# Turning written keys and normed outputs through DRAM and VectorE's 32x32 blocks, where TensorE's transposes stood

## The chip, the cores and the metric

The kernel runs on one core of one Trainium2 chip. A core has four engines that compute (TensorE, called PE in the profile, with its weight loads as PEld; VectorE, DVE; ScalarE, ACT; GpSimd, POOL), SyncE (SP), which here only issues DMAs, and 16 DMA engines that serve all queues. The metric is the device time of one execution in microseconds (us); lower is better. Beside it, a profiled execution gives the start and length of each instruction and of each DMA packet.

## What is computed

One layer of a hybrid decoder trunk over 512 tokens and 2048 channels, float32. After an RMSNorm, one product with `w_in` gives r, k, v, two small LoRA streams, a gate g, and the streams of a pooling group. The part that the change touches is the RWKV-7 group, 16 heads of 64 channels:

```python
def step(S, inp):                                   # per token, per head
    r_t, w_t, k_t, v_t, kk_t, a_t = inp
    sa = einsum('bhvk,bhk->bhv', S, -kk_t)
    S = S * w_t[:, :, None, :] + sa[..., None] * (kk_t * a_t)[:, :, None, :] + v_t[..., None] * k_t[:, :, None, :]
    y_t = einsum('bhvk,bhk->bhv', S, r_t)
...
y = head_group_norm(y, ln_w, ln_b)                  # per head, over its 64 channels
y_rwkv = (y + bonus) * silu(g_rwkv)
```

Then the pooling group, the product with `w_out` and the residual, a gated embedding (`w_pg`, `w_ple`), and a last RMSNorm.

## The kernel before

**Two kinds of work on TensorE.** Every large product is made of three matmuls of split operands (high and low halves in fp32r), 128x128 by 128x512. These are the filler: `stream()` is a generator that yields them one by one (tiles `zr`, `zk`, `zv`, `zg` for the RWKV streams, `zb` for the pooling group, `pple` for the embedding), and `pump(n)` puts n of them into the program. From line 345 on (`pin[0] = True`) TensorE keeps program order, so the filler stands exactly where `pump` is called. Between the filler stands the recurrence.

**Pairs.** The 16 heads are taken in pairs: pair j (j = 0 to 7) is 128 channels, one tile of 128 partitions by 512 tokens. A pair's tokens are cut into 8 chunks of 64. For each pair, in program order:

- `prepare(j)` (VectorE): scaled copies `ar` (reads) and `bk` (the written keys, 128 x 1024 values, 512 KB, two per token: the value key and the removal key). `bk` is a single buffer (pool `rw`, tag "bk").
- `scores(j)` (L608): 32 matmuls `pm` of `bk` with `ar`; four masked copies `mt` (L623); four DMAs of 32 KB `nd<-mt` to DRAM (L639), and from there two DMAs `n<-nd` back as a broadcast (L644).
- `invert(j)`: 31 small VectorE steps (`tm`, `xw`, L657 and L661) that solve the triangular blocks; they start with the first `n` block and are fed two at a time into the chunk loop of pair j-1, behind an instruction of its chain (`issue_after(lead[0].ins)`). Then four DMAs `xd<-xw` and four back, to `x1` (tile `x` in the profile).
- `gather(j)` (L678): the squared-key norm, decay and rate of pair j+1; four TensorE transposes `pv` of the values; **eight transposes `pbk` of `bk`** (L699) and two ScalarE copies into `bkn`, in which the tokens lie on partitions; `pump(H4)` (8), `norm_key(j+1)`, `pump(H5)` (13); **then the pending output gate of pair j-1**; `pump(HX)` (13); then the joined visit, which closes the inverse: a VectorE transpose `y` of `x1` in 32x32 blocks (L723), the matmuls `pq`, `pmv`, `px` and ScalarE copies back into `x1` and `mv`; `pump(2 * H1)` (12).
- `recur(j)` (L753): for each chunk a matmul `py` and a VectorE sum `zs` (L784), filler, a matmul `pu` and ScalarE copies `uv`, filler, a matmul `ps` with `bkn[:, ch]` and VectorE's new state `sbd` (L806), filler. Inside chunk 0, `between()` puts 20 filler matmuls, `scores(j+1)` and more filler. At the end the outputs `ysb` (tokens on partitions) are normed by eight VectorE instructions (L851), and `finish` is put into `pending`.
- `finish`, the output gate (L854): **four TensorE transposes `pyt` of `ysb`**, ScalarE's scale and bias (L860), two VectorE products with bonus and gate (L861, L862), and a DMA `yd<-yo` issued by ScalarE. The last pair's gate stands after `pump(HE)` (40).

The order of the loop is `prepare(j+1)`, `recur(j)`, `gather(j+1)`. After the last gate the pool `rw` is closed and its memory is used anew: the tiles `yin`, `yhi`, `ylo` (from L913 on), read by the product with `w_out` (`acc_o`).

**What sets the order elsewhere.** On the engines other than TensorE, and on SP's queue, the framework orders instructions when the kernel is built, taking at each point what its model of time holds ready, the earlier in the program first; so a load can stand ahead of an older one that isn't ready. Each engine then runs its list strictly in that order. SP's queue holds all weight loads (`raw`, four buffers, L129) beside `nd`, `n`, `xd` and `x`.

Of the kernel before, what the change touches and what calls it, by code (L numbers as in the profile page):

```python
# [15 lines left out]
P = 128  # L16
# [18 lines left out]
def trunk_kernel(ctx: ExitStack, tc: tile.TileContext, x, p, norm_g, w_in, mu, w0, w_up, a0, a_up,  # L35
# [84 lines left out]
    def dp(o, i):  # L120
        return dprm[:, o + i:o + i + 1]
# [455 lines left out]
    def prepare(j):  # L577
        k_, r_, v_ = need("k", j), need("r", j), need("v", j)
        pw, ipw, tha = pws.pop(j)
        kk = kks.pop(j)  # L580
        if j + 1 < NJ:
            load_ab(j + 1)


        ar = rw.tile([P, NCH // 2, 4, C], F32, name=f"ar{j}", tag="ar", bufs=2)
        bk = rw.tile([P, NCH // 2, 4, C], F32, name=f"bk{j}", tag="bk")
        k4 = kk.rearrange("p (q c t) -> p q c t", c=2, t=C)
        pw4 = pw.rearrange("p (q c) t -> p q c t", c=2)
        i4 = ipw.rearrange("p (q c) t -> p q c t", c=2)
        kp = rw.tile([P, T], F32, name=f"kp{j}", tag="kp")  # L590
        nc.vector.tensor_scalar(kp, tha, dp(33, j), dp(41, j), ALU.mult, ALU.add)
        nc.vector.tensor_tensor(kp, kp, k_, ALU.mult)
        nc.vector.tensor_scalar(tha, tha, 0.5, 0.5, ALU.mult, ALU.add)
        nc.vector.tensor_tensor(ar[:, :, 0::3, :], r_.rearrange("p (q c t) -> p q c t", c=2, t=C),
                                pw4[:, :, :, 1:C + 1], ALU.mult)
        nc.vector.tensor_tensor(bk[:, :, 0::3, :], kp.rearrange("p (q c t) -> p q c t", c=2, t=C), i4, ALU.mult)
        nc.vector.scalar_tensor_tensor(ar[:, :, 1:3, :], k_.rearrange("p (q c t) -> p q c t", c=2, t=C), dp(89, j),
                                       pw4[:, :, :, 0:C], ALU.mult, ALU.mult)
        nc.vector.tensor_tensor(kk, kk, tha, ALU.mult)
        nc.vector.tensor_tensor(bk[:, :, 1:3, :], k4, i4, ALU.mult)  # L600
        nc.vector.scalar_tensor_tensor(kp, r_, dp(49, j), kp, ALU.mult, ALU.mult)
        kph = rw.tile([P, T], F32R, name=f"kph{j}", tag="t", bufs=4)
        kpl = rw.tile([P, T], F32R, name=f"kpl{j}", tag="t", bufs=4)
        split(kph, kpl, kp)

        st_[j] = dict(pw=pw, ar=ar, bk=bk, v_=v_, kp=(kph, kpl))

    def scores(j):  # L608
        ar, bk, v_ = (st_[j][n_] for n_ in ("ar", "bk", "v_"))
        kph, kpl = st_[j].pop("kp")  # L610

        mt = rw.tile([P, 2, 8, 2, C], F32, name=f"mt{j}", tag="mt", bufs=2)
        pm = [[psM.tile([P, T], F32, name=f"pm{j}_{par}0", tag="m"),
               psY.tile([P, T], F32, name=f"pm{j}_{par}1", tag="y")] for par in range(2)]
        for par in range(2):
            for q in range(4):
                for h in range(2):
                    rows = slice(64 * h, 64 * h + 64)
                    mm(pm[par][h][:, q * P:(q + 1) * P], bk[rows, q, 2 * par:2 * par + 2, :],
                       ar[rows, q, 2 * par:2 * par + 2, :], start=True, stop=True)  # L620
        for par in range(2):
            for h in range(2):
                nc.vector.tensor_tensor(mt[:, par, h::2, :, :],  # L623
                                        pm[par][h].rearrange("p (u a t) -> p u a t", u=4, a=2),
                                        msk[:, par:par + 2, :].unsqueeze(1).to_broadcast([P, 4, 2, C]), ALU.mult)


        ps = psM.tile([P, T], F32, name=f"pbo{j}", tag="m")
        mm(ps, blk, kph, start=True, stop=False)
        mm(ps, blk, kpl, start=False, stop=True)  # L630
        bv = rw.tile([P, T], F32, name=f"bv{j}", tag="bv", bufs=2)
        nc.vector.tensor_tensor(bv, ps, v_, ALU.mult)

        nd = dram.tile([2, 2, 8, 32, 32], F32, name=f"nd{j}", tag="nd")
        for par in range(2):
            pb = 64 * (1 - par)
            for b in range(2):
                rows = slice(pb + 32 * b, pb + 32 * b + 32)
                nc.sync.dma_start(out=nd[par, b].rearrange("u r c -> r u c"),  # L639
                                  in_=mt[rows, par, :, 1 - par, 32 * b:32 * b + 32])  # L640
        nb = []
        for i in range(2):
            t_ = rw.tile([P, 16, 32], F32, name=f"n32{j}_{i}", tag=("kk", "kp")[i])
            nc.sync.dma_start(out=t_, in_=nd[:, :, :, 16 * i:16 * i + 16, :].rearrange(  # L644
                "a b u r c -> (a b u) r c").unsqueeze(0).to_broadcast([4, 32, 16, 32]))
            nb.append(t_)
        st_[j].update(mt=mt, nb=nb, bv=bv)


    def invert(j):  # L650
# [26 lines left out]

    def gather(j):  # L678
        d = st_[j]
        bk, v_, mt = d.pop("bk"), d.pop("v_"), d["mt"]  # L680
        if j + 1 < NJ:
            prepare_key(j + 1)
            decay_and_rate(j + 1)
# [7 lines left out]
        nc.scalar.copy(uv[64:128, 1::2, :], pv[64:128])  # L691


        bkn = rw.tile([P, NCH, P], F32, name=f"bkn{j}", tag="bkn")
        for hf in range(2):
            ps = psM.tile([P, T], F32, name=f"pbk{j}_{hf}", tag="m")
            for i in range(4):
                ch = 4 * hf + i
                tr(ps[:, i * P:(i + 1) * P], bk[:, ch // 2, 2 * (ch % 2):2 * (ch % 2) + 2, :], ident)  # L699
            nc.scalar.copy(bkn[:, 4 * hf:4 * hf + 4, :], ps.rearrange("p (c n) -> p c n", n=P))  # L700

        pump(H4)

        d.update(uv=uv, bkn=bkn)
        if j + 1 < NJ:
            norm_key(j + 1)
        pump(H5)
        if pending:
            pending.pop()()
        pump(HX)  # L710

        x1 = d["x1"]
# [34 lines left out]
        nc.scalar.copy(zsp[0][64:128, :].rearrange("p (h t) -> p h t", h=2), psv[64:128, 0:2, :])  # L747
        nc.scalar.copy(mv.rearrange("p q (h t) -> p (q h) t", h=2), psv)
        d["mv"] = mv
        pump(2 * H1)  # L750


    def recur(j, work, between):  # L753
        d = st_.pop(j)
        pw, ar, mt, bv, uv, bkn, mv, x1 = (d[n_] for n_ in ("pw", "ar", "mt", "bv", "uv", "bkn", "mv", "x1"))
        hop = [0]
        HC1, HC2, HC3 = HC
        lead = [None]
# [12 lines left out]
        for ch in range(NCH):  # L771
# [8 lines left out]
            if ch > 0:  # L780
# [5 lines left out]
                step()  # L786
                pump(HC1)

            psu = psS.tile([P, T], F32, name=f"pu{j}_{ch}", tag="s")
            mm(psu[:, 0:P], x1[:, 2 * q:2 * q + 2, :], zs, start=True, stop=True)  # L790
            for h in range(2):
# [58 lines left out]
        for i in range(8):  # L850
            nc.vector.tensor_scalar(y8[:, i, :], y8[:, i, :], mvr[:, i, 0:1], rs8[:, i, :],  # L851
                                    ALU.subtract, ALU.mult)

        def finish():  # L854
            sg = need("g", j)
            ps = psM.tile([P, T], F32, name=f"pyt{j}", tag="m")
            for tt in range(NT):
                tr(ps[:, tt * P:(tt + 1) * P], ysb[:, tt, :], ident)
            yo = rw.tile([P, T], F32, name=f"yo{j}", tag="t", bufs=4)
            nc.scalar.activation(yo, ps, AF.Identity, scale=dp(57, j), bias=dp(65, j))  # L860
            nc.vector.tensor_tensor(yo, yo, bv, ALU.add)  # L861
            nc.vector.tensor_tensor(yo, yo, sg, ALU.mult)  # L862
            nc.scalar.dma_start(out=yd[j], in_=yo)

        pending.append(finish)

    HC, HT, HX = (6, 9, 9), 130, 13
    HS, HN = 5, 2
    HP = 1000
    pending = []  # L870
    need("k", 0)
    need("r", 0)
    prepare_key(0)
# [11 lines left out]
    for j in range(NJ):  # L885
# [13 lines left out]
        recur(j, invert(j + 1) if j + 1 < NJ else iter(()), between)  # L899
        if j + 1 < NJ:  # L900
            gather(j + 1)
    pump(HE)
    pending.pop()()
    s2a.close()
    psB = ctx.enter_context(tc.tile_pool(name="psB", bufs=3, space=PSUM))
    lp = ctx.enter_context(tc.tile_pool(name="lp", bufs=1))
# [271 lines left out]
```

## Time and profile before

| | |
|---|---|
| runs shown | 1094.34 us median of 3 (1093.44, 1094.34, 1331.12) |
| the profiled execution | 1094.06 us, span from first to last instruction 1092.3 us |
| PE busy in the span | 98%, 6060 matmuls |
| DVE busy | 707.9 us, 65% |
| ACT busy | 448.2 us, 41% |
| mean granted TensorE clock | 0.998 |
| DMA | 138.56 MB, 178485 packets |

The span has three parts: up to about 35 us the input is normed and turned; from 35 to about 715 us the eight pairs run, with the filler between; then come `acc_o` and `acc_g`. A group row reads: line, engine, operation, tiles (out<-in), shapes, count | busy us, mean ns of one | idle us of the engine just before, and what ended it. A timeline row reads: start, length, engine, line, operation, tiles, count, and in brackets the idle time before it. A row of stretches reads: from:to, length, busy us of each engine with the number of instructions, clock, mean share of the DMA engines, GB/s. PE's lengths are modelled and overlap, so what a matmul takes of PE is the distance to the next start.

### The profile page before, as it was taken

The numbers are of one execution on the slowest core, as the hardware profiler recorded it, in microseconds if no ns is written. First come the engines' busy times: TensorE is split into PE (matmuls) and PEld (weight loads), VectorE is DVE, ScalarE is ACT, GpSimd is POOL, SyncE is SP. The second block draws the span as 40 slices with busy tenths as digits, with TensorE's granted clock in tenths as the row PEclk, the third lists the DMA queues.
The fourth block names the chain that finished last, engine by engine and source line by source line (L and its number), as shares of the span: only waits on it lengthen the run. The fifth ranks groups of instructions, "written<-read, shape, count | busy, mean of one in ns | idle before, by whom it ended". The sixth has DMA issues, their size and how long they took to land.

```text
span 1092.3 us, 17194 instructions
## 1 busy us (share of the span) xinstructions
PE 1067.4 (98%) x6060; PEld 879.1 (80%) x6060; DVE 707.9 (65%) x1835; ACT 448.2 (41%) x917; POOL 74.4 (7%) x180
## 2 busy tenths in 40 slices
PE   5999999999999999999999999999999999999996
PEld 4888878888888888787888788888888888888885
DVE  6687867878779679678886956454433424445366
ACT  7633534435335335353443344544222222233337
POOL 2100010110110110100101101000000000000000
PEclk9999999999999999999999999999999999999999
DMA  7433433332423333333334242774534438454534
GB/s 233 116 97 97 112 92 79 102 101 72 127 81 102 105 91 89 95 83 90 94 93 120 79 138 94 231 242 163 171 123 141 164 97 261 129 187 147 174 105 154
DMA packets 178485, 138.56 MB, mean 127 GB/s; under 512 B 34677, under 2 KB 139742, under 8 KB 178398
## 3 DMA queue, kind: packets, MB, share of 16 engines
q1 hardware_dynamic: 157694, 103.89, 32.2%
q10 hardware_dynamic: 20704, 33.56, 9.5%
q8 instruction: 48, 0.79, 0.3%
q14 instruction: 39, 0.32, 0.1%
HBM read 118.02 MB, written 18.87 MB: 125 GB/s over the span
## 4 chain that ended last, share of the span: by engine, by line
PE 88%; DVE 5%; DMA 3%; ACT 2%; issue 1%; SPq 0%; ACTq 0%; DVEq 0%
PE acc_o L157 16%; PE acc_g L157 16%; PE zb L157 15%; PE zv L157 8%; PE zr L157 7%; PE zg L157 7%; PE zk L157 6%; DMA n<-nd 2%; PE py L157 2%; PE pple L157 2%; PE pu L157 2%; PE pm L157 1%; PE pp L157 1%; PE ps L157 1%; PE pmv L157 1%
## 5 line engine op out<-in xcount | busy, mean ns | idle before, releaser
L133 DVE TENSOR_TENSOR wlo_g<-raw_g,whi_g 128x512 fp32r<-128x512 f32 x84 | 56.9, 683 | 78.7 <-ACT whi_g L132 78.5
L157 PE MATMUL zb<-hhi,whi_b 128*128 128x512 f32 x256 | 106.3, 415 | 0.0
L133 DVE TENSOR_TENSOR wlo_o<-raw_o,whi_o 128x512 fp32r<-128x512 f32 x64 | 43.9, 690 | 92.3 <-ACT whi_o L132 92.2
L157 PE MATMUL zb<-hhi,wlo_b 128*128 128x512 f32 x256 | 100.5, 393 | 0.0
L157 PE MATMUL acc_o<-whi_o,ylo 128*128 128x512 f32 x256 | 100.2, 391 | 0.0
L157 PE MATMUL acc_o<-whi_o,yhi 128*128 128x512 f32 x256 | 99.9, 390 | 0.0
L157 PE MATMUL zb<-hlo,whi_b 128*128 128x512 f32 x256 | 99.8, 390 | 0.0
L157 PE MATMUL acc_o<-wlo_o,yhi 128*128 128x512 f32 x256 | 99.7, 389 | 0.0
L132 ACT CAST whi_g<-raw_g 128x512 fp32r<-128x512 f32 x84 | 51.9, 620 | 105.5 <-PE acc_g L157 60.3
L157 PE MATMUL acc_g<-whi_g,x2hi 128*128 128x512 f32 x208 | 81.2, 391 | 0.0
L157 PE MATMUL acc_g<-wlo_g,x2hi 128*128 128x512 f32 x208 | 81.0, 389 | 0.0
L157 PE MATMUL acc_g<-whi_g,x2lo 128*128 128x512 f32 x208 | 80.6, 389 | 0.0
L132 ACT CAST whi_o<-raw_o 128x512 fp32r<-128x512 f32 x64 | 39.9, 623 | 97.8 <-PE acc_o L157 97.8
L813 POOL TENSOR_SCALAR s0p<-sbd,pw 64x64 f32<-64x64 f32 x96 | 56.7, 590 | 338.5 <-DVE sbd L806 253.7
L132 ACT CAST whi_b<-raw_b 128x512 fp32r<-128x512 f32 x64 | 39.7, 620 | 87.1 <-PE zv L157 34.9
L133 DVE TENSOR_TENSOR wlo_b<-raw_b,whi_b 128x512 fp32r<-128x512 f32 x64 | 43.7, 684 | 34.2 <-ACT whi_b L132 33.0
L157 PEld LDWEIGHTS zb<-hhi,wlo_b 128*128 128x128 f32 x256 | 48.0, 188 | 11.0
L661 DVE TENSOR_TENSOR xw<-xw,tm 128x60 f32<-128x60 f32 (+24 forms) x248 | 51.9, 209 | 6.8
L157 PEld LDWEIGHTS acc_o<-wlo_o,yhi 128*128 128x128 f32 x256 | 48.1, 188 | 10.0
L157 PEld LDWEIGHTS acc_o<-whi_o,ylo 128*128 128x128 f32 x256 | 48.1, 188 | 9.9
L157 PEld LDWEIGHTS acc_o<-whi_o,yhi 128*128 128x128 f32 x256 | 48.1, 188 | 9.6
L157 PEld LDWEIGHTS zb<-hhi,whi_b 128*128 128x128 f32 x256 | 48.3, 189 | 8.4
(285 smaller groups left out, 2546.8 us busy)
## 6 DMA issues: line engine op xcount, KB each, us to landing
raw_b<-in_w_in_dram SPq DMA_DIRECT2D x64, 256.0 KB
raw_o<-in_w_out_dram SPq DMA_DIRECT2D x64, 256.0 KB
raw_g<-in_w_pg_dram SPq DMA_DIRECT2D x64, 256.0 KB
raw_k<-in_w_in_dram SPq DMA_DIRECT2D x32, 256.0 KB
raw_r<-in_w_in_dram SPq DMA_DIRECT2D x32, 256.0 KB
raw_v<-in_w_in_dram SPq DMA_DIRECT2D x32, 256.0 KB
raw_g<-in_w_in_dram SPq DMA_DIRECT2D x32, 256.0 KB
n<-nd SPq DMA_DIRECT2D x16, 256.0 KB
```

Source lines behind the costliest of these rows:

```text
L132: nc.scalar.copy(hi, raw)
L133: nc.vector.tensor_tensor(lo, raw, hi.bitcast(F32), ALU.subtract)
L157: i = nc.tensor.matmul(*a, **k)
L661: nc.vector.tensor_tensor(xw[:, 0:n_, s + 1:32], xw[:, 0:n_, s + 1:32], tm[:, 0:n_, 0:w_], ALU.add)
L813: nc.gpsimd.tensor_scalar(s0p[hc, :], nxt[hc, hc], pcn[hc], None, ALU.mult)
```

## The change

Both sets of TensorE transposes are taken out. A 128x128 transpose is done in two steps instead: a DMA writes the tile to DRAM as it is; four DMAs (one for each quarter of 32 partitions) read it back with the 32x32 blocks in exchanged places, in runs of 32 floats (128 bytes); and a VectorE transpose turns each block.

- Keys: `prepare(j)` writes `bk` to DRAM (`bkd`, 512 KB). `scores(j)` reads it back behind the `n` fetch in program order, four DMAs of 128 KB, into `bg`, which takes the one buffer of tag "bk". `turn_key` turns half of it (128x512) into `bkn`, now one tile for all pairs. For pair 0 both halves are turned in `gather(0)`; for pair j+1 they are turned in `recur(j)`, at chunks 4 and 7, behind the last instruction of the chain. ScalarE's two copies into `bkn` go.
- Outputs: `recur(j)` ends with a write of the normed `ysb` to DRAM (`yb`, 256 KB). The gate is cut in two. `fetch` (where the gate stood, after `pump(H5)`) reads `yb` back with four DMAs of 64 KB into `yg`, again in the one buffer of tag "bk". `finish` (now in the middle of the old `pump(2 * H1)`, behind the joined visit) turns `yg` into `yo` on VectorE; ScalarE's scale and bias then read `yo` from SBUF instead of PSUM; the rest is as before. For the last pair `fetch` stands after 20 of the 40 filler matmuls and `finish` after all.

All new DMAs are issued by SP.

```diff
...
         kpl = rw.tile([P, T], F32R, name=f"kpl{j}", tag="t", bufs=4)
         split(kph, kpl, kp)
 
-        st_[j] = dict(pw=pw, ar=ar, bk=bk, v_=v_, kp=(kph, kpl))
+        bkd = dram.tile([P, NCH * P], F32, name=f"bkd{j}", tag="bkd")
+        nc.sync.dma_start(out=bkd, in_=bk.rearrange("p q s c -> p (q s c)"))
+        st_[j] = dict(pw=pw, ar=ar, bk=bk, bkd=bkd, v_=v_, kp=(kph, kpl))
+
+    bkn = rw.tile([P, NCH, P], F32, name="bkn")
+
+    def turn_key(j, hf):
+        cs = slice(4 * hf, 4 * hf + 4)
+        nc.vector.transpose(bkn[:, cs, :].rearrange("p c (b k) -> p (c b) k", k=32),
+                            st_[j]["bg"][:, cs, :, :].rearrange("p c b k -> p (c b) k"))
 
     def scores(j):
         ar, bk, v_ = (st_[j][n_] for n_ in ("ar", "bk", "v_"))
...
             nc.sync.dma_start(out=t_, in_=nd[:, :, :, 16 * i:16 * i + 16, :].rearrange(
                 "a b u r c -> (a b u) r c").unsqueeze(0).to_broadcast([4, 32, 16, 32]))
             nb.append(t_)
-        st_[j].update(mt=mt, nb=nb, bv=bv)
+        bg = rw.tile([P, NCH, 4, 32], F32, name=f"bg{j}", tag="bk")
+        for q in range(4):
+            nc.sync.dma_start(out=bg[32 * q:32 * q + 32],
+                              in_=st_[j]["bkd"].rearrange("(b k) (c q i) -> q k c b i", b=4, q=4, i=32)[q])
+        st_[j].update(mt=mt, nb=nb, bv=bv, bg=bg)
 
 
     def invert(j):
...
 
     def gather(j):
         d = st_[j]
-        bk, v_, mt = d.pop("bk"), d.pop("v_"), d["mt"]
+        v_, mt = d.pop("v_"), d["mt"]
         if j + 1 < NJ:
             prepare_key(j + 1)
             decay_and_rate(j + 1)
...
         nc.scalar.copy(uv[64:128, 1::2, :], pv[64:128])
 
 
-        bkn = rw.tile([P, NCH, P], F32, name=f"bkn{j}", tag="bkn")
-        for hf in range(2):
-            ps = psM.tile([P, T], F32, name=f"pbk{j}_{hf}", tag="m")
-            for i in range(4):
-                ch = 4 * hf + i
-                tr(ps[:, i * P:(i + 1) * P], bk[:, ch // 2, 2 * (ch % 2):2 * (ch % 2) + 2, :], ident)
-            nc.scalar.copy(bkn[:, 4 * hf:4 * hf + 4, :], ps.rearrange("p (c n) -> p c n", n=P))
-
+        if j == 0:
+            turn_key(0, 0)
+            turn_key(0, 1)
         pump(H4)
 
-        d.update(uv=uv, bkn=bkn)
+        d.update(uv=uv)
         if j + 1 < NJ:
             norm_key(j + 1)
         pump(H5)
         if pending:
-            pending.pop()()
+            pending[0][0]()
         pump(HX)
 
         x1 = d["x1"]
...
         nc.scalar.copy(zsp[0][64:128, :].rearrange("p (h t) -> p h t", h=2), psv[64:128, 0:2, :])
         nc.scalar.copy(mv.rearrange("p q (h t) -> p (q h) t", h=2), psv)
         d["mv"] = mv
-        pump(2 * H1)
+        pump(H1)
+        if pending:
+            pending.pop()[1]()
+        pump(H1)
 
 
     def recur(j, work, between):
         d = st_.pop(j)
-        pw, ar, mt, bv, uv, bkn, mv, x1 = (d[n_] for n_ in ("pw", "ar", "mt", "bv", "uv", "bkn", "mv", "x1"))
+        pw, ar, mt, bv, uv, mv, x1 = (d[n_] for n_ in ("pw", "ar", "mt", "bv", "uv", "mv", "x1"))
         hop = [0]
         HC1, HC2, HC3 = HC
         lead = [None]
...
                 step()
                 pump(HC1)
 
+            if ch in (4, 7) and j + 1 < NJ:
+                with tc.issue_after(lead[0].ins):
+                    turn_key(j + 1, ch // 7)
             psu = psS.tile([P, T], F32, name=f"pu{j}_{ch}", tag="s")
             mm(psu[:, 0:P], x1[:, 2 * q:2 * q + 2, :], zs, start=True, stop=True)
             for h in range(2):
...
             nc.vector.tensor_scalar(y8[:, i, :], y8[:, i, :], mvr[:, i, 0:1], rs8[:, i, :],
                                     ALU.subtract, ALU.mult)
 
+        yb = dram.tile([P, T], F32, name=f"yb{j}", tag="yb")
+        nc.sync.dma_start(out=yb, in_=ysb.rearrange("p t c -> p (t c)"))
+
+        def fetch():
+            yg = rw.tile([P, NCH, 4, 32], F32, name=f"yg{j}", tag="bk")
+            for q in range(4):
+                nc.sync.dma_start(out=yg[32 * q:32 * q + 32, 0:NT],
+                                  in_=yb.rearrange("(b k) (t q i) -> q k t b i", b=4, q=4, i=32)[q])
+            fetched.append(yg)
+
         def finish():
-            sg = need("g", j)
-            ps = psM.tile([P, T], F32, name=f"pyt{j}", tag="m")
-            for tt in range(NT):
-                tr(ps[:, tt * P:(tt + 1) * P], ysb[:, tt, :], ident)
+            sg, yg = need("g", j), fetched.pop()
             yo = rw.tile([P, T], F32, name=f"yo{j}", tag="t", bufs=4)
-            nc.scalar.activation(yo, ps, AF.Identity, scale=dp(57, j), bias=dp(65, j))
+            nc.vector.transpose(yo.rearrange("p (b k) -> p b k", k=32), yg[:, 0:NT].rearrange("p t b k -> p (t b) k"))
+            nc.scalar.activation(yo, yo, AF.Identity, scale=dp(57, j), bias=dp(65, j))
             nc.vector.tensor_tensor(yo, yo, bv, ALU.add)
             nc.vector.tensor_tensor(yo, yo, sg, ALU.mult)
             nc.scalar.dma_start(out=yd[j], in_=yo)
 
-        pending.append(finish)
+        pending.append((fetch, finish))
 
     HC, HT, HX = (6, 9, 9), 130, 13
     HS, HN = 5, 2
     HP = 1000
-    pending = []
+    pending, fetched = [], []
     need("k", 0)
     need("r", 0)
     prepare_key(0)
...
         recur(j, invert(j + 1) if j + 1 < NJ else iter(()), between)
         if j + 1 < NJ:
             gather(j + 1)
-    pump(HE)
-    pending.pop()()
+    pump(HE // 2)
+    pending[0][0]()
+    pump(HE // 2)
+    pending.pop()[1]()
     s2a.close()
     psB = ctx.enter_context(tc.tile_pool(name="psB", bufs=3, space=PSUM))
     lp = ctx.enter_context(tc.tile_pool(name="lp", bufs=1))
```

## The prediction

> **What bounds the kernel now.** I read the page's busy shares first, then the chain that ended last, then the table of stretches over the eight pairs.
>
> ```profile
> PE 1067.4 (98%) x6060; PEld 879.1 (80%) x6060; DVE 707.9 (65%) x1835; ACT 448.2 (41%) x917; POOL 74.4 (7%) x180
> PE 88%; DVE 5%; DMA 3%; ACT 2%; issue 1%; SPq 0%; ACTq 0%; DVEq 0%
> 35.00:715.00 680.00, 675.70 (x4237) 554.30 (x4236) 515.99 (x1497) 289.40 (x618) 67.92 (x126) 1.00 0.37 106
> ```
>
> TensorE is the bound: 88% of the chain, and in the 680 us of the pairs it is without work for only 4.3 us (680.00 - 675.70). So a matmul that goes is worth its own distance to the next start, and each new wait that TensorE sees costs its full length. The last row hides how uneven VectorE is. From the joined visit to the scores (`pm`) it is nearly full in some visits:
>
> ```profile
> 191.00:207.70 16.70, 16.58 (x161) 13.15 (x159) 16.54 (x28) 8.29 (x19) 2.97 (x3) 1.00 0.33 99
> ...
> 415.60:431.90 16.30, 16.30 (x161) 13.21 (x159) 16.17 (x27) 7.83 (x17) 2.09 (x3) 1.00 0.29 86
> 489.00:507.00 18.00, 16.98 (x163) 13.51 (x161) 17.88 (x30) 9.30 (x22) 1.71 (x3) 1.00 0.30 88
> ...
> sum 118.60, PE 117.46 PEld 95.03 DVE 112.01 ACT 55.24 POOL 14.36; mean PE 16.78 PEld 13.58 DVE 16.00 ACT 7.89 POOL 2.05
> ```
>
> The third number group of a row is VectorE: these three visits leave it 0.16, 0.13 and 0.12 us; the sum row is over all seven visits, which leave 6.6 us together.
>
> **1. The transposes that go.** The timeline of TensorE around one visit:
>
> ```profile
> 184.87 0.60 PE L161 MATMUL pv<-ident,sv 128*128 128x128 f32 x4
> 185.30 1.04 PE L161 MATMUL pbk<-ident,bk 128*128 128x128 f32 x8
> 186.10 0.47 PE L157 MATMUL zv<-hhi,whi_v 128*128 128x512 f32 x1
> ...
> 191.43 0.60 PE L161 MATMUL pyt<-ident,ysb 128*128 128x128 f32 x4
> 191.78 0.48 PE L157 MATMUL zb<-hhi,whi_b 128*128 128x512 f32 x1
> 192.09 0.40 PE L157 MATMUL zb<-hlo,whi_b 128*128 128x512 f32 x1
> 192.33 0.40 PE L157 MATMUL zb<-hhi,wlo_b 128*128 128x512 f32 x1
> ```
>
> Four `pv` take 0.43 us of starts, 0.108 each. Taking eight `pbk` out of the same run of transposes saves 8 x 0.108 = 0.87. The four `pyt` stand alone: 0.35 until the next start, and the matmul behind them needs 0.31 instead of 0.24 (192.09 - 191.78 against 192.33 - 192.09), so 0.42. Together 1.29 us in each of 8 pairs: **-10.3 us**. Nothing can hide this: the filler is the same count of matmuls, in the same order.
>
> The Trainium skill would make more of it: "TensorE: Matmul & The Clock Gate", section "Part 4: PE-mode transpose", gives about 275 ns for one 128x128 transpose in a kernel. The rows here have that length for one (`pbk` 273 ns, below) but starts 0.108 apart, so the trace speaks against it; with 96 transposes at the page's price the gain would be an estimated 26 us.
>
> **2. ScalarE.** It loses two copies a pair; VectorE gains three block transposes:
>
> ```profile
> L161 PE MATMUL pbk<-ident,bk x64: 272/273/329, 111.3 to 636.3; 128*128 128x128 f32 x64
> L700 ACT COPY bkn<-pbk x16: 569/590/594, 114.7 to 637.8; 128x512 f32<-128x512 f32 x16
> L723 DVE STREAM_TRANSPOSE y<-x 32x256 f32<-32x256 f32 x16 | 6.9, 430 | 1.2 <-DMA x<-xd 1.0
> L133 DVE TENSOR_TENSOR wlo_wp<-raw_wp,whi_wp 128x256 fp32r<-128x256 f32 x8 | 3.4, 422 | 1.8 <-ACT whi_wp L132 1.8
> ...
> L133 DVE TENSOR_TENSOR wlo_g<-raw_g,whi_g 128x512 fp32r<-128x512 f32 x84 | 56.9, 683 | 78.7 <-ACT whi_g L132 78.5
>   ACT x L745: 1.6, 2
> ```
>
> ScalarE is freed of 16 x 0.59 = 9.4 us, at 41% busy worth nothing by itself. But the old gate stood ahead of the joined visit, and ScalarE's copy `x` (L745), which TensorE waits for, sat twice behind the gate's output (last row, 1.6 us, from the view of who waited for `yo`). With the gate behind the visit I take **-1 us**, between -1.6 and 0.
>
> **3. VectorE.** A block transpose of 256 elements takes 430 ns, as long as a tensor operation of 256 (422); so one of 512 is taken as the 683 ns of a tensor operation of 512: three a pair, 2.05 us, 16.4 in all. Two of them (keys) stand at chunks 4 and 7, behind `zs`; they wait for `bg`, asked for three chunks earlier. There the next link, `sbd`, comes after 15 matmuls of filler (HC1 + HC2; 43.52 / 192 = 0.227 each in the `acc_o` row of part 5, so 3.4 us), which also covers the two inversion steps and a weight split queued behind `turn_key`: nothing, and 0.68 a time if that cover is full. The third (the gate's) falls into the full stretch above. There the need grows by 0.68 and TensorE's cover shrinks by the 0.42 of `pyt`: 1.1 us a visit. Three visits have no room (3 x about 1.0), the others 1.0 to 1.7. Upper end 3.3 us; lower end 0, since the norm's instructions (L851) could run earlier. I take **+2**, nearer the upper end since the full rows decide.
>
> **4. SP's queue and the inversion.** Each pair gets ten more DMAs on SP: `bkd`, `bg` x4, `yb`, `yg` x4. Where the fetch of `bg` lands in SP's list matters:
>
> ```profile
> 207.78 1.99 PE pm L157 x32
> ...
> 209.19 0.37 SPq L129 DMA_DIRECT2D raw_r<-in_w_in_dram  x1
> 211.29 1.99 SPq L639 DMA_DIRECT2D nd<-mt  x4
> 214.39 0.39 SPq L129 DMA_DIRECT2D raw_r<-in_w_in_dram  x1
> 214.97 1.16 SPq L644 DMA_DIRECT2D n<-nd  x2
> ...
> DVE tm L657 <- DMA n<-nd: 18.3, 8, 3.8
> ...
> 437.24 1.66 DMA nd<-mt
> 439.05 6.79 DMA n<-nd
> ...
> DMA packets 1053, 0.13 MB, mean 65 GB/s; under 512 B 1046, under 2 KB 1053, under 8 KB 1053
> q1 hardware_dynamic: 1053, 0.13, 39.6%
> ```
>
> `bg` may start once `pm` has read `bk` (209.77) and `bkd` has landed, so it is ready before `nd` (which waits for `mt`) though it is younger in the program; loads do overtake here (`raw_r` at 209.19 is of a later product). Then four issues of up to 0.58 us (1.16 / 2) stand ahead of `n`, 2.3 us. The holes into which they fit: 209.8 to 211.3 and 213.3 to 214.4, 2.6 us. Their data, 4096 packets of 128 bytes: the last two rows are 2 us around `nd` with almost only such packets: 0.396 x 16 x 2 us / 1053 = 12.0 ns each, so 4096 x 12.0 / 16 engines = 3.1 us. The inversion's first step waits 18.3 us for `n` over the eight pairs already, in VectorE's strict list and ahead of the chain's next `sbd`; so what `n` loses is paid nearly in full. Lower end 0 (fetch behind `n`, or all in the holes); upper end 7 x 2.3 = 16 us. I take 0.3 a pair, **+2**, since the holes are wider than the issues. `bkd` (512 KB), `yb` and the weight loads behind them: four buffers of raw weights and four of split ones, 12 matmuls (2.7 us) each, cover some 10 us; nothing, and up to 5 issues x 0.58 if that cover is gone.
>
> A rule of the Trainium skill speaks against the whole way: "VectorE: DVE Perf Modes", section "The three transpose paths", calls a plain DMA copy that turns by strides 19 times slower than the transposing DMA when the innermost stride of the destination is large. By it the time would be that of the last rival; here the innermost run stays 32 floats, and 128-byte packets cost 12.0 ns in the rows.
>
> **5. The end of the pairs.** The last gate has no loop behind it, and the tiles of the next product take over its memory:
>
> ```profile
> 691.99 3.50 DMA pled<-ple
> ...
> 709.06 0.76 DVE L851 TENSOR_SCALAR ysb<-ysb,mvr,rs 128x64 f32<-128x64 f32 x3
> ...
> 713.60 0.33 ACTq L863 DMA_DIRECT2D yd<-yo  x1
> 716.69 0.82 ACTq L915 DMA_DIRECT2D yin<-yd  x2
> 721.31 0.69 DVE L138 TENSOR_TENSOR ylo<-yin,yhi 128x512 fp32r<-128x512 f32 x1 [2.84 <-ACT yhi L137]
> 726.99 43.52 PE acc_o L157 x192
> 260.27 1.81 SPq L672 DMA_DIRECT2D x<-xd  x4
> ```
>
> Now: normed at 709.82, `yd` issued at 713.60, `yin` read 3.1 us later, its first `ylo` ready at 722.0, needed at 726.99: 5.0 us of slack. Then: `yb` issue 0.33 and landing 3.5 (as `pled`, also 256 KB), four issues 1.81 (as `x<-xd`), landing 1.66 to 3.5, transpose 0.68, ScalarE 0.59 or more (as the `bkn` copy), two products 1.37: 709.82 + 9.9 to 11.8 = 719.7 to 721.6, 6.1 to 8.0 later. Beyond 4.6 (5.0 less 0.42) that is 1.5 to 3.4; 0 if `yin` doesn't wait for the gate's memory. I take **+2**.
>
> **Sum.** The profiled execution took 1094.06 (span 1092.3 and 1.8 around it), 0.3 under the median of the runs shown. 1094.06 - 10.3 - 1 + 2 + 2 + 2 = **1088.8 us**. With all terms at their likely ends, 1085 to 1093.
>
> **Rivals.**
>
> *All hidden.* `bg` falls into the holes, VectorE's early room absorbs the gate, the memory at the end doesn't bind: 1094.06 - 10.3 - 1 = 1082.8. For it: most visits have VectorE time to spare (6.6 us). Against it: three have none.
>
> *Slower: `bg` ahead of `n`.* Where SP's list has all four fetches ahead of `nd` and the holes are not used, `n` is 2.3 us later in seven pairs; term 4 becomes 16: 1102.8. It decides from 0.3 + 5.3 / 7 = 1.05 us a pair on: from there the kernel is slower than before. For it: 18.3 us of waiting at that very place. Against: the holes.
>
> *Slower: one buffer for `bk`, `bg`, `yg`.* The next pair's `bk` (L596) can't be written before `finish` has turned `yg`.
>
> ```profile
> 338.93 1.87 DVE L851 TENSOR_SCALAR ysb<-ysb,mvr,rs 128x64 f32<-128x64 f32 x8
> 348.66 0.68 DVE L596 TENSOR_TENSOR bk<-kp,ipw 128x512 f32<-128x512 f32 x1
> ```
>
> From the norm's end to `bk` are 7.9 us; write, fetch and turn need 0.33 + 3.5 + 1.81 + 1.66 + 0.68 = 8.0, or 13.1 where the fetch lands as slowly as `n<-nd` (6.79). Behind the waiting transpose VectorE's list holds `prepare` and weight splits, for which `pm` and the filler wait; behind the fetch that waits for `yb`, SP's list holds weight loads (covered as in part 4). A visit's spare time takes about 1 us; a lateness of 2.5, half of 13.1 - 7.9, would cost 1.5 in each of six visits: 1088.8 + 9 = 1097.8.
>
> *Transposes dear.* If each took its own 273 ns of TensorE, 96 x 0.273 = 26.2: 1094.06 - 26.2 - 1 + 6 = 1072.9. The starts 0.108 apart speak against it. It is the case of the Trainium skill's page in part 1.
>
> *The fetch goes float by float.* Then 196608 packets a pair at 12.0 ns / 16 are 147 us, against 75 us a pair ((636.3 - 111.3) / 7 in the `pbk` row): 1094 + 8 x 72, over 1600 us. The diff's innermost run is 32 floats, so this hardly can be.
>
> **Chances.** Forecast 0.52, all hidden 0.19, `bg` ahead of `n` 0.16, one buffer 0.10, transposes dear 0.02, float by float 0.01. The range goes from below the all-hidden case with the whole 1.6 us of term 2 and some scatter, 1081.5, to just past the `bg` rival, 1104. A difference under about 2% (22 us) can't be told from no change by a measurement of this kernel; only the last two cases and the upper tail of the two slower ones lie beyond: faster 0.01, same 0.95, slower 0.04.
>
> **What would show it.** Right: no `pbk`, `pyt`; `acc_o` starts earlier by 3 to 9 us; STREAM_TRANSPOSE of 128x512 near 0.68 us; idle of `pu` and `py` on TensorE little changed; `tm` waiting for `n` for 18 to 21 us. Wrong: `bg` ahead of `nd` in SP's list and `tm`'s wait far over 25 us (rival two); `bk` (L596) waiting behind `yo`'s transpose (rival three); `acc_o` starting right after the filler ends with no gap (term 5); idle on TensorE ahead of `pm` in every visit (term 3 too small). If the time falls by over 11 us, I have missed a gain; if it rises, it is one of the two slower rivals.

## The result: 4% slower, and the profile after

The changed kernel took 1137.31 us (median of 6 runs, 1134.65 to 1143.75) beside 1094.73 for the kernel before: a ratio of 1.0406, interval 1.0367 to 1.0444; times 1094.7 this is 44.4 us more. The ratio is formed over executions of one state of the chip alone, without the 1331.12 us of the kernel before, so it is not the quotient of the medians. The forecast was 1088.8, in a range up to 1104. The profiled execution took 1138.62 us, its span is 1136.9 (before 1092.3), its mean clock 0.98 (before 0.998).

The page of the changed kernel: busy times, the granted clock by slices, the chain.

```profile
PE 1072.5 (94%) x5964; PEld 880.0 (77%) x5964; DVE 720.8 (63%) x1859; ACT 441.4 (39%) x901; POOL 73.2 (6%) x180
...
PEclk9999899999989999999999999998999999999999
...
PE 65%; DVE 8%; DMA 4%; issue 2%; ACT 1%; SPq 0%; ACTq 0%; DVEq 0%
```

The 96 transposes are gone (6060 matmuls to 5964), yet TensorE was busy 94% of the span, not 98%: it waits. Its share of the chain fell from 88% to 65%. The clock line has three 8s; before, the stretch of the pairs had a clock of 1.00.

To see where, I took the distance between every two successive TensorE starts, less the median distance of the same two kinds of matmul, and summed what is over 0.11 us:

| TensorE's extra distance, us | before | after |
|---|---|---|
| ahead of `py` and `pu` (steps of the recurrence) | 6.8 | 19.2 |
| ahead of `pq` (joined visit, pair 0 alone) | 0 | 8.5 |
| ahead of `pm` and `pbo` | 2.5 | 11.2 |
| ahead of the first `acc_o` | 0 | 10.3 |
| matmuls just behind a wait, at half the clock | 0 | 12.9 |
| elsewhere | 8.2 | 8.7 |

The sums are 17.5 and 70.8: 53.3 us of new waiting and slow clock. Less the 10.3 us of the transposes that went, this is 43.0, and the span grew by 44.6. So but for 1.6 us nothing else has to be looked for. The waits of TensorE, and one of VectorE, from the view of all waits (engine, tile, line <- what ended the wait: us in all, times, longest):

```profile
DVE tm L670 <- DMA n<-nd: 25.1, 8, 4.3
...
PE pu L157 <- DVE zs L795: 13.1, 9, 3.1
...
PE acc_o L157 <- ACT yhi L137: 10.1, 1, 10.1
...
PE pq L157 <- DVE y L731: 8.2, 2, 4.9
```

Before, the wait ahead of `pu` was:

```profile
PE pu L157 <- DVE zs L784: 0.7, 2, 0.4
```

**First place: `n` is late.** SP's queue in the visit whose rows before stand in the prediction (there from `nd` at 211.29 to `n` at 214.97):

```profile
219.41 0.57 SPq L658 DMA_DIRECT2D bg<-bkd  x1
220.65 0.83 SPq L648 DMA_DIRECT2D nd<-mt  x2
224.44 0.39 SPq L129 DMA_DIRECT2D raw_r<-in_w_in_dram  x1
224.88 2.63 SPq L648 DMA_DIRECT2D nd<-mt  x2
227.55 0.57 SPq L658 DMA_DIRECT2D bg<-bkd  x1
228.22 2.19 SPq L129 DMA_DIRECT2D raw_r<-in_w_in_dram  x2
230.58 1.19 SPq L653 DMA_DIRECT2D n<-nd  x2
```

From the first `nd` to the first `n` are now 9.93 us, before 3.68. Only one `bg` stands between them, 0.57 us. The rest is what else came to stand there: a `raw_r` holds the head of the queue from 221.48 (220.65 + 0.83) to 224.44, until its buffer is free, while the last two `mt` wait behind it; then the issues of these two `nd` take 2.63 us, in before's rows four took 1.99; then two more loads, 2.19. The view of SP's waits, from 217 to 232 us, has these for buffers; the longest is that of the `raw_r` at 224.44:

```profile
SPq L129 <- DVE wlo_k L133: 6.0, 3, 2.9
```

`wlo_k` is the split that reads a raw buffer and so frees it. In all eight pairs one `bg` and one or two loads stand between the last `nd` and `n`; before it was one load and nothing else. In the last seven pairs `n` was issued 10.6 to 15.2 us after the first `pm`, before 6.8 to 8.0.

The landing isn't what became slower: the inversion's first step was released 6.1 to 6.9 us after the issue of `n`, before 6.4 to 7.8.

**Behind most of these waits TensorE ran at half its clock.** Stretches around two such waits (from:to, length, busy us of PE, PEld, DVE, ACT, POOL, clock, DMA share, GB/s):

```profile
118.00:134.00 16.00, 7.78 (x111) 6.46 (x110) 13.47 (x20) 7.09 (x16) 0.40 (x1) 0.73 0.38 107
...
392.00:404.00 12.00, 8.90 (x48) 6.88 (x46) 7.26 (x30) 3.07 (x7) 1.75 (x4) 0.86 0.47 117
```

And the matmuls inside the second of them:

```profile
394.33 0.39 PE L157 MATMUL zr<-hlo,whi_r 128*128 128x512 f32 x1
394.56 0.40 PE L157 MATMUL zr<-hhi,wlo_r 128*128 128x512 f32 x1
398.05 0.49 PE L157 MATMUL pu<-zs,x 128*128 128x128 f32 x2 [3.10 <-DVE zs L795]
398.30 0.58 PE L157 MATMUL zr<-hhi,whi_r 128*128 128x512 f32 x1
398.67 0.63 PE L157 MATMUL zr<-hlo,whi_r 128*128 128x512 f32 x1
399.10 0.63 PE L157 MATMUL zr<-hhi,wlo_r 128*128 128x512 f32 x1
```

Ahead of the wait of 3.10 us the starts are 0.23 apart, behind it 0.43. The 12.9 us of the table are such matmuls.

**Second place: the end of the pairs.** SP, then VectorE, ScalarE and TensorE around the last gate:

```profile
741.80 0.34 SPq L869 DMA_DIRECT2D yb<-ysb  x1
...
747.88 1.27 SPq L874 DMA_DIRECT2D yg<-yb  x2
749.25 1.07 SPq L129 DMA_DIRECT2D raw_o<-in_w_out_dram  x2
750.37 0.57 SPq L874 DMA_DIRECT2D yg<-yb  x1
...
751.65 0.57 SPq L874 DMA_DIRECT2D yg<-yb  x1
```

```profile
755.83 0.71 DVE L881 STREAM_TRANSPOSE yo<-yg 128x512 f32<-128x512 f32 x1 [2.98 <-DMA raw_o<-in_w_out_dram]
...
758.88 0.33 ACTq L885 DMA_DIRECT2D yd<-yo  x1
...
761.54 1.95 ACTq L939 DMA_DIRECT2D yin<-yd  x4
767.80 1.72 ACT L137 CAST yhi<-yin 128x512 fp32r<-128x512 f32 x3 [7.86 <-DMA yin<-yd]
...
758.06 0.39 PE L157 MATMUL pp<-dh,wlo_wp 128*128 128x512 f32 x1
768.52 0.77 PE L157 MATMUL acc_o<-whi_o,yhi 128*128 128x512 f32 x1 [10.07 <-ACT yhi L137]
```

Before, on ScalarE:

```profile
720.66 0.62 ACT L137 CAST yhi<-yin 128x512 fp32r<-128x512 f32 x1 [2.65 <-DMA yin<-yd]
```

The norm ends where `yb` is issued. From there `yd` goes out 17.1 us later (758.88 - 741.80); before, 3.8 (713.60 - 709.82). The fetch waits 5.7 us for the write and its issues have weight loads between them; the turn waits 3.6 us more. `yin` then needs 6.3 us to be read and landed, before 4.0 (720.66 - 716.69, the first `yhi` before). TensorE stands for 10.07 us.

**Third place: `bk` behind the gate's turn.** VectorE, then TensorE, in the fifth visit:

```profile
451.63 0.70 DVE L881 STREAM_TRANSPOSE yo<-yg 128x512 f32<-128x512 f32 x1
452.37 0.69 DVE L596 TENSOR_TENSOR bk<-kp,ipw 128x512 f32<-128x512 f32 x1
452.98 0.68 DVE L600 TENSOR_TENSOR bk<-kk,ipw 128x512 f32<-128x512 f32 x1
...
453.71 2.06 PE L157 MATMUL pm<-ar,bk 64*128 64x128 f32 x32 [1.03 <-DVE bk L600]
```

The first half of `bk` is written right behind the turn, and TensorE waits 1.03 us for the second half. There were three such waits, 2.8 us together.

**What came as foreseen** is the price of the block transposes, one row each for keys and outputs:

```profile
L614 DVE STREAM_TRANSPOSE bkn<-bg 128x512 f32<-128x512 f32 x16 | 11.2, 702 | 0.0
...
L881 DVE STREAM_TRANSPOSE yo<-yg 128x512 f32<-128x512 f32 x8 | 5.7, 710 | 4.3 <-DMA raw_o<-in_w_out_dram 3.0 <-issue 1.2
```

### The profile page after: what moved, and what is told of

Its sections match the earlier page's. It is cut to its first block, busy times and chain, and to the rows that moved or that the text cites. A ratio compares the mean times of both kernels' runs of the same rounds, so it can differ in the third digit from the quotient of the medians.

```text
span 1136.9 us, 17129 instructions
## 1 busy us (share of the span) xinstructions
PE 1072.5 (94%) x5964; PEld 880.0 (77%) x5964; DVE 720.8 (63%) x1859; ACT 441.4 (39%) x901; POOL 73.2 (6%) x180
## 2 busy tenths in 40 slices
DMA packets 230965, 151.14 MB, mean 133 GB/s; under 512 B 85109, under 2 KB 190174, under 8 KB 230878
## 4 chain that ended last, share of the span: by engine, by line
PE 65%; DVE 8%; DMA 4%; issue 2%; ACT 1%; SPq 0%; ACTq 0%; DVEq 0%
PE acc_o L157 16%; PE acc_g L157 15%; PE zb L157 11%; PE zv L157 4%; PE zg L157 4%; PE zr L157 4%; DMA n<-nd 3%; PE zk L157 2%; PE pple L157 2%; PE py L157 1%; PE pu L157 1%; PE pp L157 1%; DVE tm L670 1%; DVE xw L674 1%; PE ps L157 1%
## 5 line engine op out<-in xcount | busy, mean ns | idle before, releaser
L827 POOL TENSOR_SCALAR s0p<-sbd,pw 64x64 f32<-64x64 f32 x96 | 54.4, 567 | 370.3 <-DVE sbd L820 290.6
L157 PEld LDWEIGHTS acc_o<-whi_o,yhi 128*128 128x128 f32 x256 | 48.8, 190 | 20.4 <-issue 10.5
L157 PEld LDWEIGHTS zb<-hhi,wlo_b 128*128 128x128 f32 x256 | 48.8, 190 | 11.1
L157 PEld LDWEIGHTS zb<-hlo,whi_b 128*128 128x128 f32 x256 | 48.9, 191 | 8.5
```

The costliest lines, as they stand in the source:

```text
L157: i = nc.tensor.matmul(*a, **k)
L827: nc.gpsimd.tensor_scalar(s0p[hc, :], nxt[hc, hc], pcn[hc], None, ALU.mult)
```

## The experiments

The theory after this reading: the place of `bg` in SP's list makes `n` late, and this is most of the loss (queue theory). The first rival puts the loss on the packets of the new DMAs (traffic theory); others on the last gate, on the shared buffer, or on the place of the gate. Ratios are to the kernel before, run beside each on the same chip; where two kernels are compared, it is by their ratios, a hundredth being 10.9 us.

### Each half of the change alone

`e1_keys_only` turns the keys by VectorE and leaves outputs and gate as before; `e2_outputs_only` is the other half.

```diff
 # e1: against the changed kernel
-        yb = dram.tile([P, T], F32, name=f"yb{j}", tag="yb")
...
-            nc.vector.transpose(yo.rearrange("p (b k) -> p b k", k=32), yg[:, 0:NT].rearrange("p t b k -> p (t b) k"))
-            nc.scalar.activation(yo, yo, AF.Identity, scale=dp(57, j), bias=dp(65, j))
+            ps = psM.tile([P, T], F32, name=f"pyt{j}", tag="m")
+            for tt in range(NT):
+                tr(ps[:, tt * P:(tt + 1) * P], ysb[:, tt, :], ident)
+            nc.scalar.activation(yo, ps, AF.Identity, scale=dp(57, j), bias=dp(65, j))
```

> Only the keys go through DRAM; the outputs' gate is again TensorE's, at its old place. Queue theory (the key fetch and the weight loads that slip ahead in SP's list make the n fetch late in every pair, and the wait drops TensorE's clock): n is still issued some 13 us behind the first pm (7.3 before), TensorE waits 2 to 3.5 us at the inversion's first steps in most pairs and some 8 us in pair 0's joined visit; only the gap of 10 us ahead of acc_o goes: about 1120 us. Gate theory (the split gate on VectorE and the shared buffer are the loss): no waits left, about 1087 us. Traffic theory (12 MB in 128-byte packets slow the weight loads): two thirds of the loss stays, about 1120 us, but the waits fall on the filler's weights, not on the inversion.

> Only the outputs go through DRAM; the keys are turned by TensorE as before. Queue theory: n comes as before; what is left is the gap ahead of acc_o (10 us and some 3 us of slow clock) and 0 to 3 us a visit where bk waits for the gate; 3.4 us of transposes are saved: 1104 to 1115 us. Gate theory: most of the 43 us stays, 1125 us or more.

Keys alone: 1124.36 us, ratio 1.0268 (1.0242 to 1.0294). Outputs alone: 1110.62, ratio 1.0139 (1.0124 to 1.0154). The two add up: 29.3 + 15.2 = 44.5, and the whole change costs 44.4. With the keys alone `n` is late again (issued 8.6 to 13.5 us behind the first `pm` in the last seven pairs), pair 0's visit waits 9.3 us, the half clock is there, and there is no gap ahead of `acc_o`; with the outputs alone `n` is in time and TensorE waits 11.1 us ahead of `acc_o`. So the loss has two separate sources, the keys' being the larger.

### The fetch of the keys behind `n`

```diff
-            nc.sync.dma_start(out=t_, in_=nd[...
+            nd_ = nc.sync.dma_start(out=t_, in_=nd[...
...
-        for q in range(4):
-            nc.sync.dma_start(out=bg[32 * q:32 * q + 32], ...
+        with tc.issue_after(nd_.ins):
+            for q in range(4):
+                nc.sync.dma_start(out=bg[32 * q:32 * q + 32], ...
```

> All of the change, but the key fetch is queued behind the n fetch in SP's list (order only; nothing less is moved). Queue theory: n is issued 7 to 9 us behind the first pm again, the waits at the inversion's first steps fall under 1 us a pair, pair 0's joined visit waits under 1 us; what stays is the gap ahead of acc_o and pm's waits: 1104 to 1112 us. Traffic theory: the same bytes move in the same packets, so within 6 us of 1137.

1106.48 us, ratio 1.0097 (1.0078 to 1.0116): 34 us of the 44 are gone, with as many DMAs and packets as in the changed kernel. SP's queue in the same visit:

```profile
209.44 2.59 SPq L648 DMA_DIRECT2D nd<-mt  x4
...
213.80 1.18 SPq L653 DMA_DIRECT2D n<-nd  x2
215.08 0.62 SPq L659 DMA_DIRECT2D bg<-bkd  x1
215.75 5.34 SPq L129 DMA_DIRECT2D raw_r<-in_w_in_dram  x2
```

From `nd` to `n` are 4.36 us again. The issues behind now stall instead: two loads take 5.34 us, one of them 4.10, but no step of the recurrence waits for these. Pair 0's visit has no wait left, and the recurrence's steps are back at 6.9 us of extra distance. What is left of the loss: 10.2 us ahead of `acc_o`, and 11.6 ahead of `pm` and `pbo`. The queue theory holds; that the packets make the loss wherever they stand falls.

### The same fetch on a queue of its own

That run moved the packets in time as well. Here SP's list is relieved and the fetch stays early:

```diff
-            nc.sync.dma_start(out=bg[32 * q:32 * q + 32], ...
+            nc.gpsimd.dma_start(out=bg[32 * q:32 * q + 32], ...
```

> The changed kernel with one word altered: the four fetches of `bg` are issued by GpSimd, on a queue of its own, in the place that the program gives them; SP's list is then that of before between `nd` and `n`, while the fetch's packets still move before or beside `n`. If the lateness of `n` comes from what stands ahead of it in SP's list (queue theory), `n` is issued 7 to 10.5 us behind the first `pm` and the time is that of the kernel with `bg` behind `n`, 1106.5 us, within 3. If it comes from the fetch's 4096 short packets on the DMA engines (traffic theory; 4096 x 12.0 ns / 16 = 3.1 us a pair), `n` lands 3 us later in seven pairs whatever queue issues them: 1117 to 1128 us.

1111.54 us, ratio 1.0148 (1.013 to 1.0165): neither range. `n` is issued 6.8 to 10.3 us behind the first `pm` in the last seven pairs, and 28 us come back, not 34. So with SP's list relieved most of the loss goes, though the fetch is early. But its packets did not stay the same, as the expectation had them. The page of this run has for GpSimd's queue (packets, MB, share of the 16 engines):

```profile
q0 software_dynamic: 1536, 4.20, 1.7%
```

On SP's queue the same bytes were 32768 packets of 128 bytes (the pages count 85109 packets under 512 bytes in the changed kernel, 52341 here). So early 128-byte packets beside a relieved list were not tried, and what they cost by themselves stays open. The early fetch as it went here comes with some 6 us: the recurrence's steps waited 11.6 us by the distances, 6.9 in the run above. SP's wait for the landing of `nd`, ahead of `n`, shows a part of that; first with the fetch behind `n` (the run above), then here:

```profile
SPq L653 <- DMA nd<-mt: 0.9, 1, 0.9
```

```profile
SPq L653 <- DMA nd<-mt: 3.6, 5, 1.8
```

The Trainium skill, "DMA: Bandwidth & Descriptors", section "Issuing engines are not separate DMA queues", says that DMAs from any engine end up on the same 16 DMA engines and interleave there. These rows agree: the queue was GpSimd's own, and `nd` still landed later.

### The last gate on TensorE, and both repairs

```diff
+            if j + 1 < NJ:
+                yg = fetched.pop()
...
+            else:
+                src = psM.tile([P, T], F32, name=f"pyt{j}", tag="m")
+                for tt in range(NT):
+                    tr(src[:, tt * P:(tt + 1) * P], ysb[:, tt, :], ident)
...
-    pump(HE // 2)
-    pending[0][0]()
-    pump(HE // 2)
+    pump(HE)
```

> All of the change, but the last pair's gate alone is TensorE's, at its old place. If the gap of 10 us ahead of acc_o comes from that gate's way through DRAM (written, fetched, turned, gated, stored, and only then is the memory free for yin), acc_o follows the filler without a gap and the time is 1137 - 13 = 1124 us. If the gap is the weights' (raw_o loads late behind the fetches), it stays: 1135 us or more.

1130.58 us, ratio 1.0337 (1.0306 to 1.0368), 7.5 us back and not 13. The gap ahead of `acc_o` is gone (10.3 in the table), but the recurrence's steps waited 20.7 us in place of 19.2 and pair 0's visit 10.0 in place of 8.5, though `n` was issued as far behind `pm` as before this repair (10.6 to 15.1 us). Why these waits grew stays open. With the order mended too:

> All of the change, the key fetch behind the n fetch and the last gate on TensorE; the one buffer stays. If the two effects add, 1106.5 - 13 = 1093.5 us, 1091 to 1096, about as before the change; no gap ahead of acc_o, waits of 1 to 4 us ahead of pm in three pairs. If the gap of 10 us comes back somewhere else (the filler at the end was only borrowed), 1100 us or more.

1094.49 us, ratio 1.0001 (0.9992 to 1.0011), 10.5 us under the kernel with `bg` behind `n` alone; the spans are 1105.8 and 1093.4. With these two repairs the change costs nothing and brings nothing.

### A buffer of its own for the outputs

On top of both repairs:

```diff
-            yg = rw.tile([P, NCH, 4, 32], F32, name=f"yg{j}", tag="bk")
+            yg = rw.tile([P, NT, 4, 32], F32, name=f"yg{j}", tag="t", bufs=4)
```

> All of the change, the key fetch behind the n fetch, the last gate on TensorE, and the fetched outputs in another buffer (tag t) than the keys'. One-buffer theory (bk waits until the gate has turned its fetched outputs, and pm waits for bk): pm's waits of 1 to 4 us in three pairs go, 1094 - 8 = about 1086 us. VectorE theory (the stretch ahead of pm is simply full, and 0.7 us more a visit is too much): the waits stay, within 2 us of the run without the buffer, about 1093 us.

1091.50 us (1087.45 to 1093.50), ratio 0.9969 (0.9956 to 0.9982): a little faster than the kernel before. VectorE at the same place with the shared buffer, and with its own:

```profile
429.52 0.70 DVE L885 STREAM_TRANSPOSE yo<-yg 128x512 f32<-128x512 f32 x1
430.26 0.69 DVE L596 TENSOR_TENSOR bk<-kp,ipw 128x512 f32<-128x512 f32 x1
```

```profile
418.14 0.68 DVE L596 TENSOR_TENSOR bk<-kp,ipw 128x512 f32<-128x512 f32 x1
...
423.04 0.70 DVE L885 STREAM_TRANSPOSE yo<-yg 128x512 f32<-128x512 f32 x1
423.67 0.65 DVE L600 TENSOR_TENSOR bk<-kk,ipw 128x512 f32<-128x512 f32 x1
```

With one buffer the first half of `bk` comes only when the turn has read `yg`; with two it stands 4.9 us ahead. The second half still comes behind, so only part of the wait goes: ahead of `pm` and `pbo` TensorE waits 6.7 us in place of 11.7.

The same kernel with `bg` on GpSimd's queue in place of behind `n`:

> The kernel with the order mended, the last gate on TensorE and `yg` in a buffer of its own (1091.5 us), but with the order mended by issuing `bg` from GpSimd's queue in place of standing behind `n` on SP's. If only what stands ahead of `n` on SP matters: 1091.5 us, within 2. If four issues among SP's weight loads also cost by themselves: 1088. If GpSimd's state scalings (`s0p`), queued behind a fetch that waits for `bk`'s readers, come late: 1095 or more.

1095.75 us, ratio 1.0001 (0.9986 to 1.0016), 3.5 more. The time is that of the last branch, but not for its reason: no wait of VectorE for `s0p` is in the view of waits. `nd` lands later, as in the other run with GpSimd's queue, `tm` waits 24.0 us for `n` in place of 19.2, and the recurrence's steps 11.8 in place of 7.0; SP's wait for `nd`, with `bg` behind `n` and with `bg` on its own queue:

```profile
SPq L653 <- DMA nd<-mt: 1.0, 1, 1.0
```

```profile
SPq L653 <- DMA nd<-mt: 7.1, 8, 2.3
```

### Where the keys' gain goes, and the gate's place

`e7_keys_behind_n` is the keys alone with `bg` behind `n`: 64 transposes less, 6.9 us by the prediction's price, and no known wait.

> Only the keys go through DRAM, with their fetch behind the n fetch; the gate is TensorE's at its old place. If the price of TensorE's key transposes was rightly read (0.87 us a pair) and nothing else is lost: 1095 - 7 = 1088 us, 1086 to 1090. If the packets of the fetch slow the weights or the inversion wherever they stand: 1095 us or more.

1093.02 us, ratio 0.9987 (0.9977 to 0.9996): some 1.4 us, not 6.9. `e8_gate_place` is the kernel before with nothing changed but the gate, moved behind the joined visit:

```diff
-        if pending:
-            pending.pop()()
         pump(HX)
...
-        pump(2 * H1)
+        pump(H1)
+        if pending:
+            pending.pop()()
+        pump(H1)
```

> The kernel before, with one edit: the outputs' gate, still on TensorE, stands behind the joined visit (in the middle of the 12 filler matmuls). If the old place held ScalarE's copy of x1 up, about 1 us less: 1094 us; if the new place presses on VectorE's full stretch, 0 to 5 us more.

1094.19 us, ratio 1.0 (0.999 to 1.0009): the move by itself does nothing. Both together:

> Keys by blocks with the fetch behind `n`, outputs by TensorE's transposes, and the gate moved behind the joined visit (half of `pump(2 * H1)` ahead of it). In the kernel without the move, TensorE comes to `pyt` 0.87 us earlier than before while the norm is not earlier, and waits there in four visits, 3.4 us together (0.96, 1.47, 0.74, 0.19). Theory that this is where the gain of the keys was given back: with the gate later those waits go, 1093.0 - 3.4 = 1089.6 us. Rival, that the pair's length is held by the chain of the inversion and the wait only moves to the next step: 1093.

1091.43 us, ratio 0.996 (0.9947 to 0.9973). The gate's transposes with the gate in its old place, and in the later one:

```profile
L161 PE MATMUL pyt<-ident,ysb 128*128 128x128 f32 x32 | 6.5, 286 | 1.8 <-DVE ysb L863 1.3
```

```profile
L161 PE MATMUL pyt<-ident,ysb 128*128 128x128 f32 x32 | 4.8, 272 | 0.0
```

TensorE, quicker by the eight `pbk`, had come to `pyt` before the norm was done (3.4 us by the distances of the starts, of which the row counts 1.8 as idle). With the gate later that wait is gone, and 3.0 of the expected 3.4 us come through (0.9987 to 0.996); TensorE waits ahead of `pm` and `pbo` a little more (5.5 us, 3.7 before the move). This kernel and the one with the outputs' own buffer (0.9969) are the fastest of the study, and this one is the keys' half of the change only.

## Why the prediction was wrong

**Part 1, the transposes, was right.** The starts' price, 0.108 each, closes the accounts: within 1.6 us in the changed kernel, and closely with the keys alone and the gate later, where 6.9 us of transposes less, 2.1 of new waits (19.6 in all against 17.5) make 4.8, and the span fell from 1092.3 to 1087.5. "Transposes dear" falls with it. The 275 ns that the Trainium skill, "TensorE: Matmul & The Clock Gate", section "Part 4: PE-mode transpose", gives agree with the 273 ns that one `pbk` lasts, but this length is not what one costs in a row of them. "Nothing can hide this" holds for the matmuls' time, but not for the kernel's: TensorE came earlier to producers that had not become earlier.

**Part 2, ScalarE, -1:** the gate's move alone did nothing that can be measured (1.0, 0.999 to 1.0009, so 1.1 us either way).

**Part 3, VectorE, +2:** 0.70 and 0.71 us for a transpose against the 0.68 assumed, and three visits without room, as said. But TensorE's extra distance ahead of `pm` and `pbo` grew by 8.7 us. With a buffer of its own for `yg` 6.7 us remain there, 4.2 more than before, so the term itself was about half of what it had to be, over its upper end of 3.3. The rest comes from the rival "one buffer", which acts in the same place: the own buffer took 3.5 us of the time away. I gave this rival 0.10 and +9; its mechanism was there beside the forecast's terms, not in their place.

**Part 4, SP's queue, +2, is the step that failed.** It says: "I take 0.3 a pair, **+2**, since the holes are wider than the issues", with an upper end of 2.3 a pair, four issues. I had asked which of the *new* issues could stand ahead of `n`. The runs show that these issues' own time is the small part: with the fetch in the list, weight loads whose buffers are not yet free come to stand between `nd` and `n`, the queue waits at its head, and issues behind a fetch stall. `nd` to `n` grew by 6.25 us (9.93 - 3.68) with one `bg` between. Taking `bg` out of that place brought back 34 us. The rows of before held the hint: a `raw_r` already stood between `nd` and `n`, and I read the space around it as a hole into which an issue fits, not as a place where the next load would wait. SP's waits in the trace of before show it: in the first hole SP waited 1.7 us for the first `mt`, in the second 1.0 us for that load's buffer, and what stands behind such a wait in the list can't be issued in it. Why the framework's list takes more loads there I can only argue: it counts a load as ready by its own model of time. The rival "`bg` ahead of `n`" had the right place, but not the cause: it priced four issues of 0.58 us (1102.8), where one stood there and the loads around it made the rest.

Two terms were missing altogether. Pair 0's visit has no recurrence to cover it: `n` 5.8 us later there (88.48 against 82.67 at issue) became 8.5 us of TensorE's wait. And waits cost more than their length: 12.9 us of half clock, in no term of the sum.

**Part 5, the end, +2, was mis-sized too.** `yd` came 13.3 us later (17.1 - 3.8), not 6.1 to 8.0: the write's landing took 5.7 us (747.88 less the issue's end, 742.14) where 3.5 was taken from `pled`, weight loads stood between the fetches, and the last quarter landed 3.6 after its issue. `yin` took 2.3 us longer to land as well. Counted from the norm's end the first `yhi` began 15.2 us later (26.0 against 10.8); beyond the 4.6 us of room that the prediction counted this is 10.6, near the gap of 10.2 that is there. With the half clock behind it, putting the last gate on TensorE shortened the span by 12.4 (1105.8 to 1093.4).

**The signs.** Of the "wrong" signs, `bk` behind `yo`'s transpose appeared. "No gap" at `acc_o` did not: the gap of part 5 is there, only five times as long. Idle ahead of `pm` came in three visits, not in every one. The sign for `n` appeared by half: a `bg` stood ahead of `nd` (219.41), but `tm` waited 25.1 us for `n`, where I had said "far over 25". VectorE splits weights while `n` is away, so its own wait hides most of the lateness; TensorE's wait ahead of `pu` (0.7 us for `zs` before, 13.1 after) tells it. The prediction's bound of 2%, under which a difference could not be told from no change, was too wide as well: the intervals of the ratios above reach 0.1 to 0.4% each way.

## What to carry to other kernels

A new DMA in a shared, strictly ordered queue is not priced by its own issue time: look at what else may then stand ahead of the urgent transfer, above all loads that wait for a buffer, and pin the order by hand. Where one engine is the bound, work taken from it pays only up to the next producer that has not become earlier, and a wait of a few microseconds can cost up to about twice its length where the clock falls behind it. A detour through DRAM is fit for data with a loop behind it; at a stage's end its write, fetch and turn stand bare.

## What the runs showed of the hardware

- **The clock can fall behind a wait of 2 to 3 us, and the wait's length alone does not decide.** In the changed kernel starts came 0.427 apart instead of 0.227, for some 1 to 5 us, behind waits of 2.30 to 10.2 us (by the distances of the starts) and behind one of 1.93 (at 633.50 us), but not behind one of 2.20 (at 238.58). With the last gate alone on TensorE they did not behind one of 3.29 (at 318.69), nor with the fetch on GpSimd's queue behind one of 2.98 (at 606.70). The Trainium skill, "TensorE: Matmul & The Clock Gate", section "Part 1: The HAM clock gate (the "warmup" mystery)", has the half clock (426.7 ns a start at 512 columns) after an idle window of about 3.4 us that runs freely. The spacing agrees; the length does not, since 1.93 us sufficed here.
- **An issue can stall behind queued fetches.** With `n` and a first `bg` ahead in SP's queue, the issue of a weight load took up to 4.1 us; with `bg` on GpSimd's queue, and in its packets, none of these took over 0.45. The rows, from the view of `raw_r` (ns: shortest, median, longest), with `bg` behind `n` on SP's queue and with `bg` on its own:

```profile
L129 SPq DMA_DIRECT2D raw_r<-in_w_in_dram x32: 367/373/4102, 34.2 to 506.4; - x32
```

```profile
L129 SPq DMA_DIRECT2D raw_r<-in_w_in_dram x32: 367/373/446, 33.5 to 508.2; - x32
```

- **A fetch issued by GpSimd goes in other packets, and an early one delays a small write.** The page counts 1536 packets for its 4.20 MB, where SP's queue took 32768 of 128 bytes. With both repairs and the own buffer, SP then waited for `nd` 8 times (7.1 us in all), against one wait of 1.0 with the fetch behind `n`.
- **A written tile is not back soon.** 256 KB from SBUF to DRAM and back in 128-byte runs took 14.0 us from the first issue to the turn (741.80 to 755.83), with weight loads in the same queue.
